# Ordering the first recurrent group: decay Relus and Exp placed behind weight copies, the second pair's state fetched behind a transposed x

## The chip, the cores and the metric

The kernel runs on one core of one Trainium2 chip. The metric is the time of one execution on the device in microseconds (us), as the median over several runs. The engines are named as in the profile: PE is TensorE, with PEld its weight loads, DVE is VectorE, ACT is ScalarE, POOL is GpSimd and SP is SyncE. SP, ACT and POOL also issue DMAs, each on a queue of its own.

## The reference, cut to what matters

One layer of a streaming encoder is computed for a prompt of 256 frames and for eight running streams of 16 frames, 384 tokens in all, with shared weights and a model width of 2048. A projection gives the pooling input, z, the convolution input (x, B, C), dt and gates. The part that matters here is the recurrent branch, in eight groups of eight heads:

```python
def step(h, inp):                                  # one chunk of the scan
    xc, dtc, Bc, Cc = inp
    cum = jnp.cumsum(dtc * A, axis=1)
    seg = cum[:, :, None] - cum[:, None, :]
    decay = jnp.exp(jnp.where(causal, seg, -jnp.inf))
    cb = jnp.einsum('btgn,bsgn->btsg', Cc, Bc)
    xdt = xc * dtc[..., None]
    y = jnp.einsum('btsgr,bsgrp->btgrp', cb[..., None] * decay, xdt)
    y = y + jnp.einsum('btgn,bgrpn->btgrp', Cc, h) * jnp.exp(cum)[..., None]
    last = cum[:, -1]
    w_end = jnp.exp(last[:, None] - cum)
    h = h * jnp.exp(last)[..., None, None] + jnp.einsum('bsgn,bsgr,bsgrp->bgrpn', Bc, w_end, xdt)
    return h, y
...
a_ssd = gated_rmsnorm(y, z, p['ssd_norm'])         # y * silu(z), normed per group
out = (sigmoid(gA) * (pool @ w_pool_proj) + sigmoid(gB) * (a_ssd @ w_ssd_proj)) @ w_out
```

After this come an MLP with a squared Relu and the residuals.

## The kernel before, in words

Everything is float32. Each weight tile of 128x1024 is fetched by SP (`wfetch`, L64), then cut into two parts by `wsplit`: ACT copies the rounded high part `wh` (L71), DVE subtracts to get the low part `wl` (L72). Three matmuls (L102 to L104, in `mm3`) multiply them with the two parts of the activations. A unit is one such tile, eight 128x128 blocks, so 24 matmuls; a projection tile (`proj`) is two units and 48 matmuls. The tags `w`, `wh` and `wl` have three buffers each, so the copy into a `wh` has to wait until PE is done with the unit three before it.

`take` hands out the units in the order of a queue. It cuts units until three are ready and hands out the first, so when the code asks for a unit, the two after it have been traced as cut. `cut[0]` is the latest traced ACT copy and `cut[1]` the latest traced DVE subtraction. `behind(ins)` adds an order (no wait) behind `ins` for the instructions of its block that run on the engine of `ins`. `later()` is `behind` of both `cut` instructions, `dve_later()` of the DVE one. The order on each engine is made by a scheduler when the program is built: it goes by the order of tracing, these added orders, and its own estimate of when an instruction can start. Each engine then works in that order, and an instruction that has to wait holds all behind it on that engine.

The recurrent branch is a loop over eight groups g. In a group, projection tiles come through PE as x0, B, x1, C, x2, x3, z0 to z3; in the first group (g = 0) z0 stands ahead of x3, and x0 and B were made before the loop. A convolution and a Silu (`taps`, L683 to L689) follow each x, B and C; `zproj` scales and applies Silu to each z (L1095, L1096). The accumulators of these projections alternate between two PSUM banks, which S.py, the accumulator of a pair's other products, shares.

The heads of a group are treated in two pairs, S = D.p[0] and S1 = D.p[1]. For a pair:

- `turned` transposes a finished x: DVE (L708, `turn`), four writes of POOL to DRAM (L713, `spread`), and reads back of POOL (L722 to L725 and L697, `fetch`). These three steps are run by `tick`, one after each unit of a projection; for an x there is an empty step first. The tile `xT` has a single buffer, shared by both pairs.
- `pload` fetches the state `hs` of a pair, 1 MB, on POOL's queue (L746). `cload` fetches the cumulated decay `cbc` on ACT's queue (L752).
- `xside` scales the transposed x (L865, L873), `hside` cuts it in two parts (`xhl`, `xd`; L879 to L884), `bside` does so for B (`Bhl`, `Bd`; L828 to L831), `dside` scales the state (L919).
- `eside(S, 0)` and `eside(S, 1)` are eight Relus each on ACT (L899) which write the two halves of the decay matrix `E`; `expside` takes the Exp of all of it (L908); `fside` multiplies each half with the masked product of C and B on DVE (L913).
- Then PE works through `t_pp` (L813, from `xhl` and `Bhl`), `t_yT` (L780), `t_Y` (L799, from `E` and the scaled x), `t_yi` of the second pair (L767, from its `hs`) and the state update (L928).

In the first group, before the change, the Relus of the first half are ordered behind `D.done`, the Silu of C, and the Relus of the second half, the Exp and `bside` behind `S.split`, the ACT copy in `hside`. Both states are fetched as soon as they are traced.

Of the kernel before, what the change touches and what calls it, by code (L numbers as in the profile page):

```python
# [33 lines left out]
def build(ctx, tc, io):  # L34
    nc = tc.nc
    v, s, te, gp, sy = nc.vector, nc.scalar, nc.tensor, nc.gpsimd, nc.sync
# [16 lines left out]
    def sstile(name):  # L53
        return pss.tile([P, 512], F32, tag="ss", name=name)

    def behind(ins):
        return nullcontext() if ins is None else tc.issue_after(ins.ins)
# [17 lines left out]
    def dve_later():  # L75
        return behind(cut[1])

    @contextmanager
    def later():
        with behind(cut[0]), behind(cut[1]):  # L80
            yield
# [10 lines left out]
    def even_odd(a):  # L92
        return a.rearrange("p (n a) -> p a n", a=2)

    def halves(a):
        return a.rearrange("p (a n) -> p a n", a=2)
# [40 lines left out]
    def proj(units, rhs, name, hook=None):  # L137
        o = bank[0](f"pj_{name}")[:, :T]
        for q, src in enumerate(units):
            half(o, q, take(src, f"{name}_{q}"), rhs)  # L140
            if hook:
                hook()
            tick()
        return o
# [49 lines left out]
    def three(name):  # L194
        return [sstile(f"{name}_{b}") for b in range(3)]
# [42 lines left out]
    def norm_parts(pool, sumsq, name):  # L238
        h = pool.tile([P, T], F32R, tag="nr", name=f"nh_{name}", bufs=2)
        l = pool.tile([P, T], F32R, tag="nr", name=f"nl_{name}", bufs=2)  # L240
        s.activation(h, sumsq, AF.Copy)
        v.tensor_tensor(l, sumsq, h.bitcast(F32), ALU.subtract)
        return h, l
# [25 lines left out]
    def in_units(i):  # L269
        return [win[i - 5, 0], win[i - 5, 1]]  # L270
# [408 lines left out]
    with tc.tile_pool(name="phd", bufs=2, reuse_waits="tile") as pd:  # L679
# [15 lines left out]
        def doubled(o, src):  # L695
            for q in range(2):
                gp.dma_start(o[q::2], src.rearrange("(l t) n -> t l n", l=2))  # L697
# [2 lines left out]
        gp.dma_start(d_scr, tok[:, 8])  # L700
        doubled(tokd, d_scr)

        def turned(src, i, o, od):
            xb, scr = [], t_scr[i]

            def turn():
                xb.append(pd.tile([P, T], F32, tag="xb", name=f"xb{i}"))
                v.transpose(xb[0], src)  # L708

            def spread():  # L710
                for q in range(4):
                    p32 = slice(q * 32, q * 32 + 32)
                    gp.dma_start(  # L713
                        scr[:, p32].rearrange("(j a) b -> a j b", a=32),
                        xb[0][p32].rearrange("p (j b) -> p j b", b=32),
                    )

            wait = [lambda: None] if i < 32 else []
            nb = o.shape[1]

            def fetch():
                gp.dma_start(o[:, 0], scr[:P])  # L722
                rows = scr[P : nb * P].rearrange("(b t) n -> t b n", b=nb - 1)
                gp.dma_start(o[:64, 1:], rows[64:])
                gp.dma_start(o[64:, 1:], rows[:64])  # L725
                doubled(od, scr[TP:])

            steps.append(wait + [turn, spread, fetch])

        def xturned(D, g, j):  # L730
            S = D.p[j // 2]
            if j % 2 == 0:
                S.xT = pd.tile([P, 2, 3, P], F32, tag="xT", name=f"xT{S.nm}", bufs=1)
                S.xD = pd.tile([P, 2, 2, P], F32, tag="xD", name=f"xD{S.nm}", bufs=1)
            turned(D.xs[j], g * 4 + j, S.xT[:, j % 2], S.xD[:, :, j % 2])
# [8 lines left out]
        def pload(S):  # L744
            S.hs = pd.tile([P, NB, 2 * P], F32, tag="hs", name=f"hs{S.nm}")
            gp.dma_start(S.hs, io["ssm"][S.qd])  # L746

        def cload(S):
            S.cbcs = []
            for q in range(2):  # L750
                cbc = pd.tile([P, 2, T], F32, tag="cbc", name=f"cbc{S.nm}_{q}")
                s.dma_start(cbc, cum_scr[S.h0 + q * 2 : S.h0 + q * 2 + 2, :].partition_broadcast(P))  # L752
                S.cbcs.append(cbc)
# [69 lines left out]
        def bside(D):  # L823
            D.Bhl = pd.tile([P, 2, 2, P], F32R, tag="Bhl", name=f"Bhl{D.g}", bufs=1)
            D.Bd = pd.tile([P, 2, 2, P], F32R, tag="Bd", name=f"Bd{D.g}", bufs=1)
            sign = vec[:, V_PAR + 1 : V_PAR + 2]
            with dve_later():
                s.activation(D.Bhl[:, 0], D.Bt, AF.Copy)  # L828
                v.tensor_tensor(D.Bhl[:, 1], D.Bt, D.Bhl[:, 0].bitcast(F32), ALU.subtract)
                s.activation(D.Bd[:, 0], D.BD, AF.Copy, scale=sign)  # L830
                v.scalar_tensor_tensor(  # L831
                    out=D.Bd[:, 1], in0=D.BD, scalar=sign, in1=D.Bd[:, 0].bitcast(F32), op0=ALU.mult, op1=ALU.subtract
                )
# [59 lines left out]
        def eside(S, q):  # L893
            if q == 0:
                S.E = pd.tile([P, 4, 512], F32, tag="E", name=f"E{S.nm}", bufs=1)
            for hh in (q * 2, q * 2 + 1):
                ch = S.cbcs[q][:, hh % 2]
                for row, t0, e0 in ((0, 0, 0), (9, P, P), (1, P, TP), (2, TP, T)):
                    s.activation(  # L899
                        S.E[:, hh, e0 : e0 + P],  # L900
                        ch[:, t0 : t0 + P],
                        AF.Relu,
                        bias=tok[:, row, S.h0 + hh : S.h0 + hh + 1],
                        scale=-1.0,
                    )

        def expside(S):
            s.activation(S.E, S.E, AF.Exp, scale=-1.0)  # L908

        def fside(S, h2):  # L910
            Eq = S.E[:, h2 * 2 : h2 * 2 + 2]
            with dve_later():
                v.tensor_tensor(Eq, Eq, S.D.cbm.unsqueeze(1).to_broadcast([P, 2, 512]), ALU.mult)  # L913
# [58 lines left out]
        def finish(D):  # L972
            D.bc = norm_bc(pd, D.ssum, 512, f"g{D.g}", last[0], D.parts)
# [28 lines left out]
        for g in range(G + 1):  # L1002
            if g == G:
                S = prev.p[1]
# [44 lines left out]
            D = Pair()  # L1049
# [21 lines left out]
            D.Bt = pd.tile([P, 2, P], F32, tag="Bt", name=f"Bt{g}", bufs=1)  # L1071
            D.BD = pd.tile([P, 2, P], F32, tag="BD", name=f"BD{g}", bufs=1)
            turned(D.BT, 32 + g, D.Bt, D.BD)
            if g:
                eside(prev.p[1], 1)
# [15 lines left out]
            def zproj(j):  # L1091
                ps = proj(in_units(u0 + 6 + j), xg, f"z{g}_{j}")
                z = pd.tile([P, T], F32, tag="zs", name=f"zs{g}_{j}", bufs=8)
                with later():
                    v.tensor_tensor(halves(z), even_odd(ps), halves(rstd), ALU.mult)  # L1095
                    s.activation(z, z, AF.Silu)  # L1096
                D.zs.append(z)
# [3 lines left out]
            S = D.p[0]  # L1101
# [17 lines left out]
            xturned(D, g, 2)  # L1119
            D.xs.append(conv(u0 + 5, g * 4 + 3, "xs", 6))  # L1120
            xturned(D, g, 3)
            with nullcontext() if g else behind(D.done):
                eside(S, 0)

            if g:
# [1 line left out]
            if g:  # L1127
                with later():
                    prev.parts = norm_parts(pd, prev.ssum, f"g{prev.g}")
            with nullcontext() if g else behind(S.split):  # L1130
                eside(S, 1)
                expside(S)
            cload(D.p[1])
            with nullcontext() if g else behind(S.split):
                bside(D)
            dside(S)
            zproj(1)
            if g:
                finish(prev)
            pload(D.p[1])  # L1140
            fside(S, 0)
            fside(S, 1)
            zproj(2)
            zproj(3)
            S1 = D.p[1]
            S1.py = mmtile(f"py{S1.nm}")
# [347 lines left out]
    def close_half(n):  # L1494
# [4 lines left out]
        do((merged, (0,)), (fetch, (5, 6))),  # L1499
        do((merged, (1, 2)), (fetch, (7, 8))),  # L1500
        do((turned, range(4)), (merged, (3,))),
        do((parts, range(4)), (merged, (4,)), (fetch, (9, 10, 11))),
        do((merged, (5,)), (close_half, (4,))),
# [53 lines left out]
    with tc.tile_pool(name="phf", bufs=1, side="right", reuse_waits="tile") as pf, tc.tile_pool(  # L1557
# [80 lines left out]
        for nb in range(4):  # L1638
# [3 lines left out]
            o = [sstile(f"wo{nb}_{b}") for b in range(3)] if nb else o_first  # L1642
# [168 lines left out]
    with tc.tile_pool(name="phg", bufs=1, side="right", reuse_waits="tile") as pg, tc.tile_pool(  # L1811
# [99 lines left out]
        for nb in range(2):  # L1911
            o = three(f"wd{c8}_{nb}")
# [13 lines left out]
        o = [three(f"wd{c8}_{nb}") for nb in (2, 3)]  # L1926
# [157 lines left out]
```

## Time and profile before

| what | value |
|---|---|
| median of 3 runs | 2586.57 us (2586.42 to 2587.26) |
| the profiled execution | 2585.57 us |
| its span, first to last instruction | 2583.8 us |
| mean granted TensorE clock | 0.998 |
| PE busy | 2564.7 us, 99% of the span |
| DVE, ACT, POOL busy | 2031.9, 1697.2, 466.4 us |

The profile numbers busy time by engine. Times in a timeline are us from the start of the span; a note in brackets gives how long the engine had been idle and who released it. A row of the waits gives the time in total, the number of waits and the longest. The first group runs from about 230 to 291 us.

### The profile page before, as it was taken

To read this page: it belongs to the slowest core of one execution; us is meant where nothing else is said; L and a number is where in the kernel's file an instruction comes from. 1 tells how busy PE (TensorE), PEld (TensorE's weight loads), DVE (VectorE), ACT (ScalarE), POOL (GpSimd) and SP (SyncE) were. 2 spreads that over 40 slices of the span, in tenths; PEclk is the share of its full clock that TensorE was granted. 3 is DMA by queue.
4 is the path that set the end of the run, shared out by engine and by line. 5 is a ranking of instruction groups with operands and counts; after the bars stand their busy time and mean duration, and the time that the engine had idled before them with its cause. 6 is when DMAs were issued, how large, how long until landed. Compare 5 with 4: busy or idle time off the path is not lost.

```text
span 2583.8 us, 40108 instructions
## 1 busy us (share of the span) xinstructions
PE 2564.7 (99%) x14953; PEld 2388.4 (92%) x14953; DVE 2031.9 (79%) x2843; ACT 1697.2 (66%) x2683; POOL 466.4 (18%) x695
## 2 busy tenths in 40 slices
PE   9999999999999999999999999999999999999998
PEld 9999999999999988888888888999999999999997
DVE  6887799999999966798888855767777777777778
ACT  6545666666756546868888634666676666666665
POOL 0113345444544412211111100000000000000000
PEclk9999999999999999999999999999999999999999
DMA  7667566676767659977666555655555554555544
GB/s 286 208 218 246 197 221 230 212 248 212 237 228 241 216 189 306 294 226 225 199 184 205 186 171 195 198 162 155 154 157 166 165 167 147 155 155 165 160 157 155
DMA packets 150098, 516.57 MB, mean 200 GB/s; under 512 B 22432, under 2 KB 25312, under 8 KB 144656
## 3 DMA queue, kind: packets, MB, share of 16 engines
q1 hardware_dynamic: 98944, 355.14, 40.6%
q0 software_dynamic: 43904, 144.07, 19.3%
q10 hardware_dynamic: 7056, 14.81, 1.8%
q8 instruction: 117, 1.92, 0.3%
q14 instruction: 77, 0.63, 0.1%
HBM read 453.57 MB, written 60.36 MB: 199 GB/s over the span
## 4 chain that ended last, share of the span: by engine, by line
PE 84%; issue 7%; DVE 4%; DMA 2%; ACT 2%; POOL 1%; DVEq 0%; SPq 0%; POOLq 0%; ACTq 0%
PE pj_up L102 6%; PE pj_up L103 6%; PE pj_up L104 6%; PE wd L1245 6%; PE wd L1246 6%; PE wd L1244 6%; PE pj_x L102 4%; PE pj_x L103 4%; PE pj_x L104 4%; PE pj_z L104 3%; PE pj_z L102 3%; PE pj_z L103 3%; PE sq L1245 3%; PE sq L1246 3%; PE sq L1244 3%
## 5 line engine op out<-in xcount | busy, mean ns | idle before, releaser
L71 ACT ACTIVATE wh_up<-w_up 128x1024 fp32r<-128x1024 f32 x126 | 133.1, 1057 | 219.4 <-PE pj_up L103 202.7
L102 PE MATMUL pj_x<-xgh,wh_x 128*128 128x384 f32 x768 | 251.9, 328 | 0.9 <-DVE zs L1095 0.9
L102 PE MATMUL pj_up<-x1h,wh_up 128*128 128x384 f32 x768 | 250.5, 326 | 0.0
L103 PE MATMUL pj_x<-xgl,wh_x 128*128 128x384 f32 x768 | 250.4, 326 | 0.0
L104 PE MATMUL pj_x<-xgh,wl_x 128*128 128x384 f32 x768 | 250.4, 326 | 0.0
L103 PE MATMUL pj_up<-x1l,wh_up 128*128 128x384 f32 x768 | 250.4, 326 | 0.0
L104 PE MATMUL pj_up<-x1h,wl_up 128*128 128x384 f32 x768 | 250.4, 326 | 0.0
L72 DVE TENSOR_TENSOR wl_up<-w_up,wh_up 128x1024 fp32r<-128x1024 f32 x126 | 154.1, 1223 | 54.3 <-ACT wh_up L71 54.3
L1204 POOL DMA_DIRECT2D w_b_wd<-w_down x30 | 25.3, 843 | 832.9 <-DMA w_b_wd<-w_down 318.5
L102 PE MATMUL pj_z<-xgh,wh_z 128*128 128x384 f32 x512 | 167.8, 328 | 2.9 <-ACT wh_z L71 2.9
L104 PE MATMUL pj_z<-xgh,wl_z 128*128 128x384 f32 x512 | 167.6, 327 | 0.7 <-DVE wl_z L72 0.7
L103 PE MATMUL pj_z<-xgl,wh_z 128*128 128x384 f32 x512 | 167.6, 327 | 0.0
L102 PEld LDWEIGHTS pj_x<-xgh,wh_x 128*128 128x128 f32 x768 | 145.1, 189 | 3.0 <-DVE zs L1095 1.3
L103 PEld LDWEIGHTS pj_up<-x1l,wh_up 128*128 128x128 f32 x768 | 145.2, 189 | 1.2
L102 PEld LDWEIGHTS pj_up<-x1h,wh_up 128*128 128x128 f32 x768 | 145.2, 189 | 1.2
L103 PEld LDWEIGHTS pj_x<-xgl,wh_x 128*128 128x128 f32 x768 | 145.2, 189 | 0.0
L104 PEld LDWEIGHTS pj_x<-xgh,wl_x 128*128 128x128 f32 x768 | 145.2, 189 | 0.0
L104 PEld LDWEIGHTS pj_up<-x1h,wl_up 128*128 128x128 f32 x768 | 145.2, 189 | 0.0
L71 ACT ACTIVATE wh_x<-w_x 128x1024 fp32r<-128x1024 f32 x96 | 100.4, 1052 | 61.8 <-PE pj_z L103 31.6
L1221 ACT COPY acc<-wd 128x512 f32<-128x512 f32 x214 | 124.7, 583 | 23.8 <-PE wd L1246 23.8
L1244 PE MATMUL wd<-wh_b_wd,fh 128*128 128x512 f32 x360 | 136.4, 379 | 0.0
L1245 PE MATMUL wd<-wl_b_wd,fh 128*128 128x512 f32 x360 | 136.4, 379 | 0.0
(495 smaller groups left out, 8171.9 us busy)
## 6 DMA issues: line engine op xcount, KB each, us to landing
w_up<-w_up SPq DMA_DIRECT2D x128, 512.0 KB, 4.1
w_b_wd<-w_down SPq DMA_DIRECT2D x120, 512.0 KB, 4.3
w_x<-w_in SPq DMA_DIRECT2D x96, 512.0 KB, 3.8
w_z<-w_in SPq DMA_DIRECT2D x64, 512.0 KB, 4.1
w_b_sq<-w_ssd SPq DMA_DIRECT2D x64, 512.0 KB, 5.2
w_ga<-w_ga SPq DMA_DIRECT2D x32, 512.0 KB, 3.4
hs<-ssm POOLq DMA_DIRECT2D x16, 1024.0 KB, 6.2
new_ssm_s<-hs POOLq DMA_DIRECT2D x16, 1024.0 KB, 4.4
```

What stands on the lines that cost most here:

```text
L71: cut[0] = s.activation(h, w, AF.Copy)
L72: cut[1] = v.tensor_tensor(l, w, h.bitcast(F32), ALU.subtract)
L102: te.matmul(out, wh, xh, start=first, stop=False, **how)
L103: te.matmul(out, wh, xl, start=False, stop=False, **how)
L104: return te.matmul(out, wl, xh, start=False, stop=last, **how)
L1204: summed[0] = gp.dma_start(w, unit(0, np_ * 2), accum_op=ALU.add)
L1221: s.copy(dst, o)
L1244: te.matmul(out, mh, vh, start=begin, stop=False, skip_group_check=held)
L1245: te.matmul(out, mh, vl, start=False, stop=False, skip_group_check=held)
L1246: te.matmul(out, ml, vh, start=False, stop=end, skip_group_check=held)
```

## The change

For the first group alone:

- The Relus of the first half are ordered behind the latest traced cuts at that point (`later()`) instead of behind the Silu of C. The latest cut there is that of z1's second unit.
- The Relus of the second half and `bside` are traced after z1's projection and ordered behind the latest cuts there, those of z2's second unit. The Exp is traced after z2's projection and ordered behind the cuts of z3's second unit; the two `fside` follow it. `cload` of the second pair is now traced ahead of the second half's Relus.
- The second pair's state fetch is ordered, on POOL, behind the last of the three `xT` fetches that has been traced by then. After z1's projection that is the fetch of x2: of the empty step, the transpose, the writes and the fetch, x2 has had all four by then, and x3 two.

```diff
+        xfetched = []
...
-                gp.dma_start(o[64:, 1:], rows[:64])
+                sent = gp.dma_start(o[64:, 1:], rows[:64])
                 doubled(od, scr[TP:])
+                if i < 32:
+                    xfetched.append(sent)
...
-            with nullcontext() if g else behind(D.done):
+            with nullcontext() if g else later():
                 eside(S, 0)
...
-            with nullcontext() if g else behind(S.split):
+            if g:
                 eside(S, 1)
                 expside(S)
             cload(D.p[1])
-            with nullcontext() if g else behind(S.split):
+            if g:
                 bside(D)
             dside(S)
             zproj(1)
             if g:
                 finish(prev)
-            pload(D.p[1])
-            fside(S, 0)
-            fside(S, 1)
+            else:
+                with later():
+                    eside(S, 1)
+                    bside(D)
+            with nullcontext() if g else behind(xfetched[-1]):
+                pload(D.p[1])
+            if g:
+                fside(S, 0)
+                fside(S, 1)
             zproj(2)
+            if not g:
+                with later():
+                    expside(S)
+                fside(S, 0)
+                fside(S, 1)
             zproj(3)
```

## The prediction

> **What bounds the kernel now.** I read the page first, for the engine that fills the span. Its row of busy times says that PE does:
>
> ```profile
> PE 2564.7 (99%) x14953; PEld 2388.4 (92%) x14953; DVE 2031.9 (79%) x2843; ACT 1697.2 (66%) x2683; POOL 466.4 (18%) x695
> ```
>
> So an edit to the order of ACT, DVE and POOL is worth only what it gives back of PE's waits and of PE's clock. Second, the waits of PE in the first 290 us, which end with the first group (engine, who waited, for whom: us in total, times, longest):
>
> ```profile
> PE pj_z L102 <- ACT wh_z L71: 2.9, 1, 2.9
> PE warm_o L291 <- DVE warm L287: 1.2, 1, 1.2
> PE pj_x L102 <- DVE zs L1095: 0.9, 1, 0.9
> PE pj_z L104 <- DVE wl_z L72: 0.7, 1, 0.7
> ```
>
> Three of these rows belong to the first group. Third, PE's own timeline around them (start, duration, and in brackets the idle time before and who ended it):
>
> ```profile
> 250.21 0.43 PE L102 MATMUL pj_x<-xgh,wh_x 128*128 128x384 f32 x1 [0.86 <-DVE zs L1095]
> 250.48 0.33 PE L103 MATMUL pj_x<-xgl,wh_x 128*128 128x384 f32 x1
> 250.64 0.33 PE L104 MATMUL pj_x<-xgh,wl_x 128*128 128x384 f32 x1
> ...
> 273.55 0.33 PE L104 MATMUL pj_z<-xgh,wl_z 128*128 128x384 f32 x1
> 276.79 0.43 PE L102 MATMUL pj_z<-xgh,wh_z 128*128 128x384 f32 x1 [2.91 <-ACT wh_z L71]
> 277.06 0.33 PE L103 MATMUL pj_z<-xgl,wh_z 128*128 128x384 f32 x1
> 278.05 0.43 PE L104 MATMUL pj_z<-xgh,wl_z 128*128 128x384 f32 x1 [0.67 <-DVE wl_z L72]
> ...
> 287.31 0.83 PE L813 MATMUL py<-xhl,Bhl 128*128 128x256 f32 x6
> 287.98 0.38 PE L780 MATMUL Y<-cst,yis 128*128 128x128 f32 x2
> ```
>
> x3, z1 and z2 are 3 x 48 = 144 matmuls. From the third (250.64) to the last (273.55) are 141 steps in 22.91 us, so 0.1625 us a step, without a break. z3 should begin at 273.71 and `t_pp` one tile later, at 273.55 + 49 x 0.1625 = 281.51. It begins at 287.31: this place costs **5.80 us**, more than the waits named. The waits hold 273.71 to 276.79 (3.08), 0.83 on the third matmul, and 0.11 on each of two restarts, 4.13 together. The other 1.67 is clock. A view by stretches shows it (stretch, its length, then PE, PEld, DVE, ACT and POOL busy, the granted clock, DMA share, GB/s):
>
> ```profile
> 274.00:278.00 4.00, 0.59 (x2) 0.30 (x2) 3.58 (x5) 3.99 (x5) 1.96 (x4) 1.00 0.18 41
> 278.00:282.00 4.00, 3.95 (x15) 3.95 (x16) 2.73 (x3) 1.26 (x3) 1.98 (x4) 0.60 0.75 235
> ```
>
> The clock falls to 0.60 just after the gap, and 15 matmul records lie in 4 us where 0.1625 a step gives 24 or 25. Fourth, ACT's timeline, for what it did while PE waited for its copy:
>
> ```profile
> 242.90 2.44 ACT L899 ACTIVATE E<-cbc,tok 128x128 f32<-128x128 f32 x8
> ...
> 262.05 1.06 ACT L71 ACTIVATE wh_z<-w_z 128x1024 fp32r<-128x1024 f32 x1 [1.80 <-PE pj_z L103]
> 265.95 0.63 ACT L879 ACTIVATE xhl<-xT 128x512 fp32r<-128x512 f32 x1 [2.84 <-DVE xT L865]
> 266.55 0.63 ACT L883 ACTIVATE xd<-xD 128x512 fp32r<-128x512 f32 x1
> 267.09 0.60 ACT L689 ACTIVATE xs<-cacc,vec 128x384 f32<-128x384 f32 x1
> 267.60 2.43 ACT L899 ACTIVATE E<-cbc,tok 128x128 f32<-128x128 f32 x8
> 269.93 0.40 ACT L828 ACTIVATE Bhl<-Bt 128x256 fp32r<-128x256 f32 x1
> 270.07 0.33 ACTq L752 DMA_DIRECT2D cbc<-cum_scr  x1
> 270.35 1.28 ACT L908 ACT_TABLE_LOAD   x1
> 271.64 1.91 ACT L908 ACTIVATE E<-E 128x2048 f32<-128x2048 f32 x1
> 273.46 0.49 ACT L830 ACTIVATE Bd<-BD,vec 128x256 fp32r<-128x256 f32 x1
> 273.97 1.28 ACT L1096 ACT_TABLE_LOAD   x1
> 275.27 0.52 ACT L1096 ACTIVATE zs<-zs 128x384 f32<-128x384 f32 x1
> 275.70 1.99 ACT L71 ACTIVATE wh_z<-w_z 128x1024 fp32r<-128x1024 f32 x2
> ```
>
> The two copies at 275.70 are z3's. The first needs only the buffer that z1's second unit frees at 265.9 (144 - 48 matmuls after 250.2). It comes 9.8 us later, behind an unbroken line that starts with the wait for the transposed x1 and holds eight Relus, two table loads and the Exp.
>
> **The change, part by part.** *The Exp behind z3's second copy.* This edge can't be missed: the Exp, its table load and what follows can no longer stand ahead of z3's copies. The second copy is free to run when z2's first unit is done, 24 steps after 265.9, at 269.8. What may still stand between z2's copy (ends 263.1) and z3's two: eight Relus 2.43, Bhl 0.40, Bd 0.49, xhl 0.63, xd 0.63, x3's Silu 0.60, z1's Silu 0.52 and the copies themselves 1.99, in all 7.7 us in the 10.6 us until 273.71. Even if xhl waits until 265.95 as now, Relus and `bside` fill that hole and 4.4 us follow it. The copies end by about 271; the cover is 2 to 3 us, and without it PE waits again, microsecond for microsecond. I count all of 5.80 back: 4.13 of waits, 1.67 of clock.
>
> *What is late next: the Exp itself.* It is 1.28 + 1.91, then two multiplications on DVE, before `t_Y`. In the new time `t_Y` comes at 281.51 + 0.67 (287.31 to 287.98 in the rows) or just after.
>
> ```profile
> 273.59 2.36 DVE L913 TENSOR_TENSOR E<-E,cbm 128x1024 f32<-128x1024 f32 x2 [2.80 <-ACT E L908]
> ```
>
> From 271.0: 1.28 + 1.91 + 2.36 gives 276.6, 5.6 us early. If the scheduler puts z2's Silu first, whose input ends at 273.9: the scaling (about as long as that Silu), Silu 0.52 and the same 5.55 give 280.5, 1.7 us early. So I cost it at nothing. The number of table loads stays: Silu to Exp and back once.
>
> *The first Relus go from 242.90 to behind z1's second copy.* That copy is free to run 24 steps into x3, at 254.2, and ends at 255.3; the next has to wait for x3's end, at 258.1. The Relus, 2.44, fit between and cost nothing there. What they leave is 2.44 us ahead of x3's second copy and of x2's convolution. Behind these on DVE stood the scaling of z0, for whose bank x3 waited 0.86, or 0.97 with the restart (250.48 - 250.21 against 0.1625). Bounds: 0 if DVE keeps its late order, 0.97 if it all moves; a loss has no source, as nothing is put ahead of that scaling. I take 0.8, near the upper end, since the wait is shorter than the 2.44 us freed ahead of it.
>
> *`cload` of the second pair.* Two transfers on ACT's queue, traced ahead of the second Relus whose buffer the second needs, so it still issues behind them (270.07 now, about 266 then). Its first reader comes after `t_Y`: nothing. *`bside`* on DVE, two subtractions (an estimate of half a microsecond each, from ACT's 0.40 and 0.49 on the same tiles), moves behind z2's cut: Bhl is read at 281.5, 15 us later: nothing. *`fside`* keeps its work; costed above.
>
> *The state fetch on POOL's queue.* One issue, 1 MB, moves from the group's beginning to behind the third `xT` fetch of x2. POOL's timeline, then the time of the 16 state fetches from issue to landing (min/median/max), first of all of them, then of those issued between 291 and 940 us:
>
> ```profile
> 268.56 0.58 POOL L722 DMA_DIRECT2D xT<-t_scr  x1 [4.43 <-DVE xhl L880]
> 269.12 0.61 POOL L724 DMA_DIRECT2D xT<-t_scr  x1
> 269.72 0.60 POOL L725 DMA_DIRECT2D xT<-t_scr  x1
> ```
>
> ```profile
> DMA to landing us min/median/max: 5.3/6.2/13.2
> ```
>
> ```profile
> DMA to landing us min/median/max: 5.3/6.0/7.0
> ```
>
> What it leaves: the fetches and transposes of x0, B and x1 run without 1 MB beside them, so the scaled x1, for which xhl waits 2.84, comes earlier by up to that; it only widens the cover above. What it joins: it issues at about 271.5, behind x2's two remaining reads, and lands at 276.8 to 284.7, 277.7 by the median. The state is read by `t_yi`, behind `t_Y` and so after 282.2. Median: 4.5 us early; longest: up to 2.5 us late. I take nothing, by the median, since the long one is of the beginning, where both states come at once, and the rows of stretches above show 41 and 235 GB/s at the new place. Queued behind it on POOL are x3's transposed writes and reads, now from 271.5 on, which the second pair's scaling wants only behind `t_Y`; a few us of delay fit. SP's queue isn't touched; its weight buffers come free earlier, with the cuts.
>
> **The sum.** 5.80 + 0.8 = 6.6 us off the profiled execution's 2585.57, so 2579.0. That execution lies 1.0 below the median of the runs, 2586.57; carried over, **2580.0**. The view of waits has no row of PE between 291 and 940 us that could take the gain up again. As tell-apart for this kernel I take 0.2%, 5.2 us: faster means under 2581.4.
>
> **A rule against it.** The clock fell after a gap of about 3.1 us. If that slow stretch is not the gap's doing and stays, only 4.13 + 0.8 = 4.9 come back: 2581.7, just within 0.2%. For: the gap is short. Against: the rows show 1.00 until the gap and 0.60 behind it. Chance 0.05. The Trainium skill, "TensorE: Matmul & The Clock Gate", section "HAM oscillation — how this bites in real kernels", has the clock drop for idle gaps over about 3.4 us; by that, this gap should not have been enough. The trace disagrees so far as one gap can show.
>
> **The rivals.** *The Exp turns into the new wait, at `t_Y`.* If z2's Silu and then x0's next weight copy (0.99 a piece, half of 1.99) stand ahead of the Exp, E is ready at 281.5, and with a DVE cut between, about 282.7, against 281.4 to 282.2: 0.5 to 1.3 us lost, 2581 to 2581.5; I put it at 2581.5. For: ACT's order is the scheduler's guess. Against: the Exp can start 4 us before z2's Silu. Chance 0.10.
>
> *Nothing changes at the place that counts.* z3's copies stay behind ACT work that waits, now for x1 or for z1's scaling on DVE. Time as before, 2586.6, or half of it. For: ACT did wait 2.84 for xT. Against: the 7.7 us above. Chance 0.07.
>
> *Slower: the state arrives late.* Place: `t_yi` of the second pair, all of PE queued behind it. It eats the gain once the state lands 6.6 us after 282.2, and decides for slower by 0.2% from 294, which is 22 us after its issue, or less if x2's fetch is late itself. For: that fetch hangs on xhl through the single `xT`. Against: 13.2 was the longest of 16. At 25 us: 282.2 becomes 296.5, 14.3 lost, so 2594. Chance 0.06.
>
> **How the numbers follow.** The forecast has the remaining 0.72, at 2580.0; its own range is 2578.6 (all 0.97, and the 1.0 between profile and median being clock that comes back too) to 2581.4. The range of 8 in 10 reaches on to partial waits of about 3 us: 2578.6 to 2583.0. Faster is the forecast, 0.72; same is 0.05 + 0.10 + 0.07 = 0.22; slower 0.06.
>
> **What would show it.** PE without a wait for `wh_z` or `wl_z` and a granted clock of 1.00 from 250 to 290; `t_pp` some 6 us earlier; on ACT, Relus right behind the z copies and the Exp's table load behind z3's; the wait for `zs` gone or under 0.2; the second state fetch on POOL behind the reads of x2, with a landing under 8 us. Wrong would be a PE wait at L799 or L767, or a wait for `wh_x` in the next group.

## The result, and the profile after

| | before | after |
|---|---|---|
| median | 2583.78 us (18 runs, 2581.56 to 2587.26) | 2579.59 us (18 runs, 2578.30 to 2581.29) |
| the profiled execution | 2585.57 us, span 2583.8 | 2579.85 us, span 2578.1 |

The ratio is 0.9984, 95% interval 0.9977 to 0.9990: 4.2 us faster. That is inside the 0.2% which the prediction took as the least that it would call faster. Two things stand out beside it. The three runs that the prediction started from (2586.42 to 2587.26) lie at the upper end of this kernel's runs: no other of the 18 is above 2585.26. And the runs of the kernel before are spread over 5.7 us, those of the changed one over 3.0.

PE's waits in the first 290 us after the change (engine, who waited, for whom: total, times, longest); both rows of z3 are gone, the row of x3 is not:

```profile
PE warm_o L291 <- DVE warm L287: 1.2, 1, 1.2
PE pj_x L102 <- DVE zs L1099: 0.9, 1, 0.9
PE pj_p L367 <- ACT xgh L327: 0.3, 1, 0.3
```

PE's timeline after the change, the first matmul of x3 and the first of `t_pp`:

```profile
250.64 0.43 PE L102 MATMUL pj_x<-xgh,wh_x 128*128 128x384 f32 x1 [0.89 <-DVE zs L1099]
...
281.94 0.83 PE L817 MATMUL py<-xhl,Bhl 128*128 128x256 f32 x6
```

They are 31.30 us apart, as an unbroken run should have them; before it was 37.10. ACT's timeline after, which shows why:

```profile
255.75 2.44 ACT L903 ACTIVATE E<-cbc,tok 128x128 f32<-128x128 f32 x8
...
264.49 2.43 ACT L903 ACTIVATE E<-cbc,tok 128x128 f32<-128x128 f32 x8
...
268.45 1.04 ACT L71 ACTIVATE wh_z<-w_z 128x1024 fp32r<-128x1024 f32 x1
269.40 0.20 ACT L443 COPY cbuf<-cstate 128x24 f32<-128x24 f32 x1
270.28 1.06 ACT L71 ACTIVATE wh_z<-w_z 128x1024 fp32r<-128x1024 f32 x1 [0.68 <-PE pj_z L103]
271.36 1.28 ACT L912 ACT_TABLE_LOAD   x1
272.65 1.92 ACT L912 ACTIVATE E<-E 128x2048 f32<-128x2048 f32 x1
274.47 1.04 ACT L71 ACTIVATE wh_x<-w_x 128x1024 fp32r<-128x1024 f32 x1
```

z3's first copy stands at 268.45 instead of 275.70, its second waits only for its buffer, and the Exp comes behind both. In the view by stretches (PE, PEld, DVE, ACT, POOL busy, granted clock, DMA share, GB/s) PE runs through, at full clock:

```profile
274.00:278.00 4.00, 4.00 (x26) 4.00 (x26) 3.40 (x4) 3.32 (x4) 0.00 (x0) 1.00 0.77 290
278.00:282.00 4.00, 4.00 (x27) 4.00 (x26) 1.78 (x2) 1.06 (x1) 2.99 (x5) 1.00 0.62 195
```

From `t_pp` to the end of the span are 2296.5 us before (2583.8 - 287.31) and 2296.2 after (2578.1 - 281.94): nothing was given back later. So this pair of executions shows 5.7 us, not far from the 6.6 forecast, while the many runs show 4.2. The experiments had to tell why.

### The profile page after: what moved, and what is told of

Read it like the earlier page. It is cut to its first block, busy times and chain, and to the rows that moved or that the text cites. A ratio compares the mean times of both kernels' runs of the same rounds, so it can differ in the third digit from the quotient of the medians.

```text
span 2578.1 us, 40110 instructions
## 1 busy us (share of the span) xinstructions
PE 2562.9 (99%) x14953; PEld 2387.1 (93%) x14953; DVE 2031.0 (79%) x2843; ACT 1696.9 (66%) x2683; POOL 466.5 (18%) x695
## 4 chain that ended last, share of the span: by engine, by line
PE 91%; DVE 4%; issue 2%; ACT 1%; DMA 1%; POOL 0%; SPq 0%; DVEq 0%; ACTq 0%; POOLq 0%
PE pj_up L102 6%; PE pj_up L104 6%; PE pj_up L103 6%; PE wd L1260 6%; PE wd L1261 6%; PE wd L1259 6%; PE pj_x L102 5%; PE pj_x L103 5%; PE pj_x L104 5%; PE pj_z L104 3%; PE pj_z L103 3%; PE pj_z L102 3%; PE sq L1260 3%; PE sq L1261 3%; PE sq L1259 3%
```

## The experiments

Kernels that share a chip below were timed side by side and share the runs of the kernel before.

**The kernel before, unchanged**, for its spread (first chip).

> The kernel before, unchanged, beside itself. Theory A (the clock falls behind the 3.1 us gap in some executions only, so that a usual execution loses the 4.1 us of waits at z3 and only some lose the further 1.7 us of slow clock): ratio 1.000; the waits for z3's weights are again 2.9 and 0.7 us, t_pp comes between 35.4 us (31.30 + 4.13) and 38.8 us (3.4 us more of half clock) behind x3's first matmul, and need not come at the 37.10 of the first profile. Theory B (the clock falls every time, and what the medians lack of the forecast was given back later in the kernel): again 37.1, with a granted clock of 0.60 behind the gap.

> One more look at the kernel before. Theory A: the waits as before, the length of the slow stretch different from run to run (0 to 3.4 us of half clock, so t_pp 35.4 to 38.8 us behind x3's first matmul). Theory B: 37.1 each time.

Measured: before_again 2583.18 us against 2583.73 of the shared runs, ratio 0.9994 (0.9985 to 1.0003). PE's waits between 240 and 290 us in its profile, then in that of before_look_2:

```profile
PE pj_x L102 <- DVE zs L1095: 1.8, 1, 1.8
PE pj_z L102 <- ACT wh_z L71: 1.4, 1, 1.4
PE pj_z L104 <- DVE wl_z L72: 0.7, 1, 0.7
```

```profile
PE pj_x L102 <- DVE zs L1095: 1.2, 1, 1.2
PE pj_z L102 <- ACT wh_z L71: 1.1, 1, 1.1
PE pj_z L104 <- DVE wl_z L72: 0.7, 1, 0.7
```

The clock stayed at 1.00 in both. So theory B falls: the clock does not fall every time. Theory A was right on the clock and wrong on the waits, which were to be 2.9 again: z3's wait is 1.4 and 1.1, and x3's is longer than the 0.9 of the first profile. `t_pp` comes 33.9 and 33.6 us behind x3's first matmul, under the 35.4 that was the least expected. Both waits move from execution to execution.

**The two halves alone** (same chip). The new order on ACT with `pload` as before:

```diff
-            with nullcontext() if g else behind(xfetched[-1]):
-                pload(D.p[1])
+            pload(D.p[1])
```

> The new order of Relus and Exp, with the second state fetched at the beginning as before. If the order on ACT is what counts: no PE wait for z3's weights, t_pp 31.3 us behind x3's first matmul, ratio to before 0.9984 as with the whole change; xhl waits for the transposed x1 until about 266 and z3's first copy starts at about 271, still 2 us early. Rival (the earlier x1 is what counts): a wait of 1 us or more for z3's weights stays, ratio 0.9992 or higher.

and the kernel before with that line alone taken over:

```diff
-            pload(D.p[1])
+            with nullcontext() if g else behind(xfetched[-1]):
+                pload(D.p[1])
```

> The second state's fetch moved, Relus and Exp as before. If the order on ACT is what counts: x1 comes some 3 us earlier, the line of Relus, table load and Exp starts with it and now stands ahead of z2's second copy instead of z3's first; PE waits there, about 2 to 3 us for wh_z and less than 1 for wl_z, and the ratio is 0.9988 to 1.0005. Rival (the earlier x1 is what counts): no wait over 1 us, ratio 0.9984.

Measured: Relus and Exp alone 2581.53 us, 0.9991 (0.9982 to 1.0000); the state alone 2584.37 us, 1.0002 (0.9993 to 1.0011). With the state alone, ACT's line of Relus and Exp began earlier and came to stand ahead of z2's second copy, which then started at 269.80; the wait moved there as expected, 1.6 us long instead of 2 to 3. PE's timeline of it, and two stretches:

```profile
270.89 0.43 PE L102 MATMUL pj_z<-xgh,wh_z 128*128 128x384 f32 x1 [1.56 <-ACT wh_z L71]
...
272.15 0.43 PE L104 MATMUL pj_z<-xgh,wl_z 128*128 128x384 f32 x1 [0.67 <-DVE wl_z L72]
```

```profile
270.00:274.00 4.00, 2.44 (x9) 2.15 (x10) 3.54 (x5) 3.98 (x4) 1.36 (x3) 0.82 0.94 293
274.00:278.00 4.00, 4.00 (x20) 4.00 (x19) 3.39 (x4) 1.07 (x4) 1.21 (x3) 0.75 0.54 185
```

The clock fell here too. So the earlier x1 gains nothing by itself. With Relus and Exp alone z3 has no wait, as expected, but the gain is about half of the whole change's (0.9991 where 0.9984 was expected), and x3 has the longest wait so far, 2.4 us, with a granted clock of 0.57 behind it. What held it is on DVE: the scaling of z0, for whose bank x3 waits, stands behind the transpose of x1, and that waits for the four transposed writes of an earlier tile. DVE in before_again, where both states are fetched at the beginning; then the time from issue to landing of the two states (issued at 229.70 and 230.24) and of those four writes (issued from 235.07 to 237.25):

```profile
246.82 0.58 DVE L708 STREAM_TRANSPOSE xb<-xs 128x384 f32<-128x384 f32 x1 [1.83 <-DMA t_scr<-xb]
...
250.77 0.52 DVE L1095 TENSOR_TENSOR zs<-pj_z,rstd 128x384 f32<-128x384 f32 x1
```

```profile
DMA to landing us min/median/max: 12.2/13.5/14.8
DMA to landing us min/median/max: 9.5/10.1/10.4
```

After the change, the one early state (issued at 229.91), the same four writes (from 235.28 to 237.12), and DVE:

```profile
DMA to landing us min/median/max: 11.3/11.3/11.3
DMA to landing us min/median/max: 5.2/5.7/6.3
```

```profile
244.36 0.57 DVE L710 STREAM_TRANSPOSE xb<-xs 128x384 f32<-128x384 f32 x1
...
249.56 0.58 DVE L710 STREAM_TRANSPOSE xb<-xs 128x384 f32<-128x384 f32 x1 [0.68 <-ACT xs L689]
250.06 0.52 DVE L1099 TENSOR_TENSOR zs<-pj_z,rstd 128x384 f32<-128x384 f32 x1
```

The writes are issued behind the states on POOL's queue and land only after them. In before_again the second state lands at 245.0, the last of the four writes at 246.7, and the transpose starts at 246.82. In all eight profiles with both states at the beginning, the first of the four writes lands 0.5 us after the second state, and the transpose starts 0.1 us after the last. After the change the early state lands at 241.2 and the writes by 242.3, 2 us before DVE comes to the transpose at 244.36. So the writes wait for the states, DVE for the writes, and PE for DVE. (POOL itself also waits for each state before an issue, at 242.17 and 245.27 in before_again, but these are the last two writes of the next tile, which x1's transpose does not need.) With the second state moved, DVE's wait is gone. In all profiles of this study DVE waited there 0.3 to 2.7 us in seven of the eight with both states at the beginning, and not at all in the six with the second one moved.

**The kernel before, once more** (second chip), for how the two waits hang together.

> A further look at the kernel before. If z3's copy hangs on the landing of the transposed x1 and PE's arrival on x3's wait: z3's wait is the end of its first copy less the end of z2 (31.3 - 7.8 = 23.5 us behind x3's first matmul), within 0.2 us, so that a longer wait at x3 goes with a shorter one at z3; slow clock only where z3's wait is near 3 us. Rival: z3's wait is 2.9 us with a slow stretch whatever x3's wait was.

PE's waits between 240 and 290 us, and the stretch behind x3's:

```profile
PE pj_x L102 <- DVE zs L1095: 2.6, 1, 2.6
PE pj_z L104 <- DVE wl_z L72: 0.7, 1, 0.7
```

```profile
252.00:256.00 4.00, 3.90 (x15) 3.90 (x16) 2.78 (x6) 0.52 (x1) 4.00 (x8) 0.62 0.86 291
```

x3 waits 2.6 us, and z3's wait for `wh_z` has shrunk out of the list: its copy ends at 277.2, when PE, late by x3 and its slow clock, has just got there. z3's copy starts at 275.70, 275.32, 274.67 and 276.14 in the four profiles, a range of 1.5 us; PE gets to z3 at 273.9, 275.0, 274.7 and 277.2, a range of 3.3. In the first three, ACT's line ahead of the copy waits for the landing of the transposed x1; here it does not, but follows z2's copy at 265.37, which waited 1.82 us for PE. What x3 loses, z3 largely saves. By the expected formula a wait of 1.6 us (277.2 less 252.10 + 23.5) should have been left at z3; the slow clock at x3 made PE later by that. The slow clock came with x3's wait this time, not with z3's near 3 us, so that part of the expectation was wrong.

The four profiles of before against three of the whole change, from the start of the first pair's `t_yi` (L767) to `t_pp`:

| | before | before_again | before_look_2 | before_look_3 | after | after_again | same_chip_whole |
|---|---|---|---|---|---|---|---|
| x3's wait | 0.9 | 1.8 | 1.2 | 2.6 | 0.9 | 0 | 0.4 |
| z3's waits | 2.9 + 0.7 | 1.4 + 0.7 | 1.1 + 0.7 | 0.7 | 0 | 0 | 0 |
| slow clock | at z3 | no | no | at x3 | no | no | no |
| `t_yi` to `t_pp`, us | 39.05 | 36.80 | 35.91 | 37.70 | 33.28 | 32.33 | 32.79 |

The means are 37.4 and 32.8: 4.6 us, in the interval of the runs.

**The Exp alone, and the whole change again** (second chip). Only `expside` and the two `fside` move:

```diff
                 eside(S, 1)
-                expside(S)
+                if g:
+                    expside(S)
...
-            fside(S, 0)
-            fside(S, 1)
+            if g:
+                fside(S, 0)
+                fside(S, 1)
             zproj(2)
+            if not g:
+                with later():
+                    expside(S)
+                fside(S, 0)
+                fside(S, 1)
```

> Only the Exp and its two multiplications move behind z3's cuts; the Relus, the cut of B and both state fetches stay as before. If the two table loads and the Exp (4.5 us) are what made z3's copy late: it starts at about 271 to 271.5, no wait at z3, and the ratio is that of Relus and Exp together, 0.9991. Rival (the Relus, 2.4 us, are needed too): a wait of about 1 us stays at z3 and the ratio is 0.9995 or more. x3's wait stays 0.9 to 1.8 us in both.

> The changed kernel again, beside the one before and the variant. If the change's worth is the waits of a usual execution of the kernel before (2 to 4 us at x3 and z3 together, the slow clock only in some): ratio 0.9984, x3's wait 0.9 us again, none at z3, t_pp 31.3 us behind x3's first matmul. Rival (the forecast of 6.6 us was right and the first comparison unlucky): ratio 0.9975.

Measured: the Exp alone 2579.93 us, 0.9987 (0.9978 to 0.9996), no wait at z3, its first copy at 270.81; x3 waits 0.9. The whole change 2579.85 us, 0.9983 (0.9975 to 0.9992). The Exp and its table loads are enough for z3; the rival that the Relus are needed too falls. The ratio of the whole repeats, though the forecast's 0.9975 is just inside its interval. x3 had no wait here, against an expected 0.9.

**z0's scaling ahead of x2's transpose**, on top of the whole change (second chip). After the change DVE no longer waits for writes ahead of that scaling, but 0.68 us for x2's Silu:

```diff
-                v.transpose(xb[0], src)
+                with behind(scaled[0] if i == 2 else None):
+                    v.transpose(xb[0], src)
...
-                    v.tensor_tensor(halves(z), even_odd(ps), halves(rstd), ALU.mult)
+                    scaled[0] = v.tensor_tensor(halves(z), even_odd(ps), halves(rstd), ALU.mult)
```

> The changed kernel with one more order: x2's transpose on DVE (which waits for x2's Silu) stands behind the scaling of z0 instead of ahead of it. If that transpose is what holds the bank that x3 waits for: x3's wait goes from 0.9 us to under 0.2, no wait at z3, and 0.9 us come off the time of the changed kernel on the same chip, some 0.04%. Rival (the bank or PE's clock holds x3 in another way, or z1's first cut, now behind three small DVE instructions, becomes late): x3's wait stays or moves to z1, no gain.

Measured 2578.75 us, ratio to before 0.9978 (0.9970 to 0.9987), 1.1 us under the whole change on this chip. DVE and PE in its profile:

```profile
246.54 0.56 DVE L1100 TENSOR_TENSOR zs<-pj_z,rstd 128x384 f32<-128x384 f32 x1
247.30 0.58 DVE L711 STREAM_TRANSPOSE xb<-xs 128x384 f32<-128x384 f32 x1 [0.21 <-ACT xs L689]
```

```profile
247.85 0.43 PE L102 MATMUL pj_x<-xgh,wh_x 128*128 128x384 f32 x1
...
279.15 0.83 PE L818 MATMUL py<-xhl,Bhl 128*128 128x256 f32 x6
```

The bank is free at 247.1, before PE asks for it, and PE runs from x3 to `t_pp` without a wait.

**The four side by side on a third chip**, to size the parts.

> The whole change, once more, on one chip with its parts. Expected 2579.8 us as in both earlier comparisons; DVE does not wait for the transposed writes between 240 and 252 us, x3 waits 0 to 0.9 us, no wait at z3.

> Relus and Exp moved, both states fetched at the beginning. If the second state's early fetch holds back the transposed writes, which DVE's transpose of x1 waits for, ahead of z0's scaling and so of x3: DVE waits 0.3 to 2.7 us there, x3 waits 0.9 to 2.6, and the median is 1 to 2 us over the whole change. Rival (the state's place is worth nothing, as the prediction priced it): the same median as the whole change within 0.5 us.

> The Exp alone moved. If the Exp with its two table loads is all that z3 needs: no wait at z3, the median that of Relus and Exp together within 0.7 us, and 1 to 2 us over the whole change. Rival (the Relus' place matters too): the median 1 us or more over Relus and Exp together.

> The whole change and z0's scaling ahead of x2's transpose. Expected 1 us under the whole change (2578.8), x3 without a wait. Rival (the first difference was chance): the same median as the whole change within 0.4 us.

| kernel | median, us | ratio to before | x3's wait, us |
|---|---|---|---|
| before | 2583.87 | 1 | |
| the Exp alone | 2580.48 | 0.9987 (0.9978 to 0.9996) | 1.4 |
| Relus and Exp | 2581.03 | 0.9993 (0.9984 to 1.0002) | 1.8 |
| the whole change | 2579.44 | 0.9983 (0.9974 to 0.9992) | 0.4 |
| the whole, z0 first | 2578.85 | 0.9980 (0.9971 to 0.9989) | 0 |

Adding the state's move to Relus and Exp is worth 1.6 us in the medians (1.9 in the means, 0.7 to 3.2 at 95%): the rival that it is worth nothing falls. Relus and Exp against the Exp alone differ by 0.7 in the means, -0.8 to 2.3, so the Relus' place is not shown to matter either way. The whole change beats the Exp alone by 0.8 in the means on the second chip and by 1.2 here, over both by 1.0 (0.2 to 1.9). The Exp and the state moved with the Relus in their old place were not run. In same_chip_exp DVE did not wait for the writes, the one such profile of eight, and x3 still waited 1.4, for x2's transpose and z0's scaling. z0 first beats the whole change by 0.6 here, less than the 1 us expected; over both chips, 22 runs each, by 1.1 in the means (0.5 to 1.7). It is the fastest version of this study.

## Why the prediction was right or wrong

**The place and the mechanism: right.** z3's copies came out from behind the Relus, the table loads and the Exp; PE passes z3 without a wait and at full clock. The first Relus fit ahead of z2's copy (255.75, forecast 255.3), z3's copies are done at 271.3 (about 271), and E is ready at 277.4, 5.5 us ahead of its reader (5.6). The Exp alone does this.

**The term of 5.80 us: mis-sized.** "I count all of 5.80 back: 4.13 of waits, 1.67 of clock" took one execution for all. Measured in the same way, x3's first matmul to `t_pp` less 31.30, the other three profiles give 2.6, 2.3 and 2.7 (the last with a slow clock at x3 in it, not z3), 3.3 in the mean of the four. The step that failed is the one that carried a gap of one profile to the median. The gap is the difference of two things that do not move together: an ACT line that in three of the four profiles hangs on a DMA's landing, and PE's arrival, which hangs on x3's wait. The one profile had x3's shortest wait of the four and so z3's longest.

**The absolute time: right by luck in part.** 2580.0 against 2579.6 came of a start that was 2.8 us high (2586.57 against 2583.78) and a gain that was 2.4 us large (6.6 against 4.2); the two errors nearly cancel.

**The first Relus' 0.8 us: wrong in its cause.** The 2.44 us freed on ACT did not bring z0's scaling forward in the pair of profiles (0.86 before, 0.89 after), because DVE's order keeps x2's transpose, and with it x2's Silu, ahead of it. The order that puts z0 first shows this. That "a loss has no source" was wrong too. With the Relus moved, DVE's order has x3's second subtraction ahead of the last step of x2's convolution. DVE before, then after:

```profile
246.16 1.93 DVE L685 SCALAR_TENSOR_TENSOR cacc<-cbuf,vec,cacc 128x384 f32<-128x384 f32 x3 [0.21 <-ACT cacc L683]
248.01 1.22 DVE L72 TENSOR_TENSOR wl_x<-w_x,wh_x 128x1024 fp32r<-128x1024 f32 x1
```

```profile
247.13 1.22 DVE L72 TENSOR_TENSOR wl_x<-w_x,wh_x 128x1024 fp32r<-128x1024 f32 x1
248.26 0.62 DVE L685 SCALAR_TENSOR_TENSOR cacc<-cbuf,vec,cacc 128x384 f32<-128x384 f32 x1
```

So x2's Silu comes late, and DVE waits 0.68 us for it ahead of z0's scaling. That wait is in all five profiles of the whole change and of Relus and Exp alone, and in none with the Relus in their old place. x3's time from `t_yi` did fall, from 3.7, 2.9, 2.3 and 2.0 to 2.0, 1.0 and 1.5 us, which is 1.2 in the mean. That comes with the state's move: it is 1.0 with the state alone, and 3.5 and 2.9 with Relus and Exp alone.

**The state's move at nothing: wrong.** That it "only widens the cover above" missed what the early fetch held back: the transposed writes behind it on POOL's queue, DVE's transpose that waits for them, z0's scaling behind that, and x3. Its new place is free, as forecast: issued at 268.67, landed 7.3 us later, with no wait of PE for it.

**The rivals.** The Exp at `t_Y` and the late state did not come. "Nothing changes at the place that counts" did not come for the whole, but its mechanism, a line of ACT that holds z's copies, is what the state alone does, at z2. That the slow stretch is not the gap's doing was half right: it is the doing of a wait, but of some waits only, so that its 1.67 us do not belong into a usual execution's sum.

**The rule against it.** The granted clock fell behind waits of 2.9, 2.6 and 2.4 us, and behind 1.6 followed by 0.7, but not behind 1.8 (twice) or behind 1.4 followed by 0.7. The Trainium skill, "TensorE: Matmul & The Clock Gate", section "HAM oscillation — how this bites in real kernels", speaks of idle gaps over about 3.4 us. All of these waits are shorter, so the trace disagrees. The length of a wait does not sort the cases; PE's busy time in windows of 3.41 us does. All four slow stretches are 3.41 us at a granted clock of 0.50, and each starts a whole number of such windows after the clock's first entry in the trace, from which PE is at full pace (in the first profile 13 matmuls in the window before 9.16 and 23 in the next). There 79 windows lie between 9.16 and 278.82; in the others it is 71, 72 and 77. In the first profile the window ahead of the fall and the fall; then in before_again, by the same count, the window with the wait of 1.8 us and the next:

```profile
275.40:278.82 3.42, 1.36 (x7) 1.07 (x8) 3.00 (x4) 3.34 (x5) 1.82 (x4) 1.00 0.13 34
278.82:282.23 3.41, 3.41 (x12) 3.41 (x12) 1.91 (x3) 0.52 (x1) 1.16 (x2) 0.50 0.86 273
```

```profile
248.50:251.91 3.41, 1.61 (x20) 1.00 (x20) 3.38 (x6) 2.09 (x3) 2.84 (x6) 1.00 0.58 166
251.91:255.33 3.42, 3.42 (x23) 3.42 (x22) 2.11 (x5) 0.00 (x0) 3.42 (x6) 1.00 0.92 310
```

Ahead of the four falls PE was busy 1.36, 1.26, 1.29 and 1.18 us of the window. In all fourteen profiles, cut into windows in this way, every window with 1.36 us or less was followed by half the clock, and none with 1.6 or more. This is read from the profiles afterwards; no run shifted a wait against the windows to test it. The same page of the Trainium skill, section "What's actually happening", has a window of 3413 ns that is not reset when a kernel starts. The trace agrees with its length. That section of the Trainium skill has the clock at half after at least one idle window. Here 1.2 to 1.4 us of work in the window did not keep the clock up.

## What to carry to other kernels

A wait on the bounding engine is the difference between its arrival and another chain's; where that chain hangs on DMAs, take several executions before its size goes into a sum, and reckon with an early stall on the same engine taking up part of it. An instruction that an engine reaches too early holds all behind it: a transpose that waits for writes to land cost PE time through the unrelated scaling behind it. A fetch of 1 MB that is not yet needed is not free on its queue: writes of 48 KB issued 5 us behind it landed only after it. And a new order for one engine can change that of another, as the Relus' place on ACT did on DVE.

## What the runs showed of the hardware

The clock: each slow stretch lasted 3.41 us at a granted clock of 0.50 (0.32 us from one matmul to the next instead of 0.16), and came after a window of 3.41 us in which PE was busy for 1.36 us or less. The DMAs: with both states at the beginning their fetches took 11.2 and 13.2 us in the first profile, the one fetched later 7.3. Four writes of 48 KB behind two states took 9.5 to 10.4 us to land in before_again, behind one state 5.2 to 6.3 us after the change.
